# Ten blocks by seven products instead of nine, with the ordinary work spread evenly over their half units

## The chip, the cores and the metric

The kernel runs on one core of a Trainium2 chip. The metric is the device time of one execution in microseconds; the median of several runs is compared. TensorE (PE in the profile) multiplies, VectorE (DVE) and ScalarE (ACT) do elementwise work, GpSimd (POOL) and SyncE (SP) issue transfers.

## The reference

Two decoder layers on x of 256 tokens by 2048, in float32. Each layer mixes tokens (a gated unit and windowed attention), and then comes the part that matters here, a gated feed-forward of width 5632:

```python
h2 = rms_norm(x, norm2_g[l])
x = x + (jax.nn.silu(h2 @ w_gate[l]) * (h2 @ w_up[l])) @ w_down[l]
```

## The kernel before, in words

**Three products for one.** Each float32 weight tile is split into a rounded high half `wh` (a cast on ScalarE, L95) and the rest `wl` (a subtraction on VectorE, L96), in `split2`. The activations are split likewise when they are made. `mm3` (L133) then issues three matmuls of 128x512: high by high (L134), high by low (L135), low by high (L136). There are five buffers of `wh`, four of `wl`, seven of `raw`, the weights as loaded by `raw_load` through SP's queue.

**Ordinary units.** `unit` loads one weight tile of 256 rows by 512 columns, splits it and multiplies it with both token halves: 12 matmuls, one split. In the feed-forward an ordinary gate-and-up block of 512 columns (`gate_up`, through `even`) is 16 units, 8 for w_gate and 8 for w_up; the down product (`down`) of one block is 8 units, over the four column blocks of the output, and two or three blocks are gathered in one pass of `down`. These accumulate in the two PSUM banks of the pool `pd`. `down` starts each output block with a ScalarE copy of the residual into PSUM (L686) and ends it with a copy back (L705).

**Blocks by seven products.** `seven(b)` computes gate and up of a block together. The two token halves, the two halves of the contraction and the pair gate/up make a product of 2x2 by 2x2 sub-matrices, which Winograd's form does with seven products instead of eight. Its half units, `s_unit`, have 6 matmuls and one split each. Five PSUM banks of the pool `pa` hold the five running results (`bank[0]` to `bank[4]`). Sums of weight tiles are made by VectorE (L605, L606, L611; 128x1024 each) and in one case by a transfer that adds while it writes (L613, issued by GpSimd); sums of activations are made once per layer in `combine`. In the first part four rounds of five half units are issued; then the banks are combined on VectorE (L624 to L629); in the second part four rounds of two half units add the products with `b21` to bank 0 and with the kept tiles `t2` to bank 2. At the end L638 adds bank 2 to `m0`, ScalarE applies silu (L641), VectorE gates (L643), and `act_later` has the result transposed two and three ticks later (`act_T`: four transposes, a cast at L554, a subtraction at L555). A tick is one ordinary unit or two half units.

**The order.** Instructions are issued from Python in the order of two generators. `s_stream` gives the half units of all blocks in `S_BLOCKS` and yields after each, and once more after the sums from PSUM and after the end of a block: 30 times per block. `std_stream` gives the ordinary units: `gate_up` of the other blocks, and `down` as soon as two blocks have their transposed pairs (`CHUNK`); it yields False if nothing is ready. A planner joins them: `vec` adds the assumed VectorE time of what was issued to `debt`, `pe` takes off the assumed TensorE time times `LOAD`, and after each half unit ordinary units are issued while the debt is positive:

```python
for _ in s_stream():
    while debt[0] > 0.0 and next(other, False):
        pass
```

What is left of the ordinary units follows after the last block. The tile framework then places the instructions on the engines; its order on one engine can differ from the order of issue.

Of the kernel before, what the change touches and what calls it, by code (L numbers as in the profile page):

```python
# [12 lines left out]
F32 = mybir.dt.float32  # L13
# [3 lines left out]
ALU = mybir.AluOpType  # L17
# [3 lines left out]
P = 128  # L21
D = 2048
SEQ = 256
NTOK = SEQ // P
# [10 lines left out]
NB = 512  # L35
# [3 lines left out]
NI = 3584 // NB  # L39
NFF = DFF // NB  # L40
ND = D // NB
S_BLOCKS = (2, 3, 4, 5, 6, 7, 8, 9, 10)
GU_BLOCKS = tuple(b for b in range(NFF) if b not in S_BLOCKS)
CHUNK = (2, 3)
ACT_TILES = 8
VEC = 1.14
VEC_P = 0.6
MM = 0.227
LOAD = 0.93
WARM = 12  # L50
UNIT_AT = (6, 9, 12, 15, 19, 23)

# [12 lines left out]
def trunk(ctx, tc, x, xt, w_in, w_out, w_gate, w_up, w_down, sgu_w, sgu_g, consts,  # L65
          band, out):
    nc = tc.nc
# [4 lines left out]
    zp = ctx.enter_context(tc.tile_pool(name="zp", bufs=8))  # L72
# [6 lines left out]
    def f(t):  # L79
        return t.bitcast(F32)  # L80

    def raw_load(src, parts=1):
        raw = wp.tile([P, 2, NB], F32, tag="raw", name="raw", bufs=7)
        n = 2 // parts
        for i in range(parts):
            nc.sync.dma_start(raw[:, i * n : (i + 1) * n, :], src[:, i * n : (i + 1) * n, :])
        return raw

    def split2(raw):
        wh = wp.tile([P, 2, NB], F32R, tag="wh", name="wh", bufs=5)  # L90
        wl = wp.tile([P, 2, NB], F32R, tag="wl", name="wl", bufs=4)
        step = 2 if clock[0] > 1 else 1
        for j in range(0, 2, step):
            src = raw[:, j : j + step, :]
            nc.scalar.copy(wh[:, j : j + step, :], src)  # L95
            nc.vector.tensor_tensor(  # L96
                wl[:, j : j + step, :], src, f(wh[:, j : j + step, :]), ALU.subtract
            )
        vec(1)
        return wh, wl  # L100

    clock = [0]
    debt = [0.0]

    def vec(n, cost=VEC):
        debt[0] += n * cost

    def pe(n):
        debt[0] -= n * MM * LOAD

    serial = itertools.count()
    pending = []

# [3 lines left out]
    def tick(w=1.0):  # L117
        clock[0] += w
        due = sorted((e for e in pending if e[0] <= clock[0]), key=lambda e: e[:2])
        pending[:] = [e for e in pending if e[0] > clock[0]]  # L120
        for e in due:
            e[2]()
# [10 lines left out]
    def mm3(acc, ah, al, wh, wl, first, last, again=False):  # L133
        nc.tensor.matmul(acc, ah, wh, start=first, stop=False, skip_group_check=again)  # L134
        nc.tensor.matmul(acc, ah, wl, start=False, stop=False, skip_group_check=again)  # L135
        nc.tensor.matmul(acc, al, wh, start=False, stop=last, skip_group_check=again)  # L136

    def unit(src, acts, acc, first, last, again=False):
        raw = raw_load(src, 2 if clock[0] < 4 else 1)
        wh, wl = split2(raw)  # L140
        for j in range(2):
            act, aj = acts[j]
            for t in range(NTOK):
                ts = slice(t * P, (t + 1) * P)
                mm3(
                    acc[t], act[:, 0, aj, ts], act[:, 1, aj, ts], wh[:, j, :], wl[:, j, :],
                    first and j == 0, last and j == 1, again,
                )
        pe(12)
        tick()  # L150

    def product(srcs, pairs):
# [98 lines left out]
    for lay in range(L):  # L251
# [298 lines left out]
        def act_T(b, c, sg, pairs_f=pairs_f):  # L550
            ps = pm.tile([P, 2, SEQ], F32, tag="sm", name="ps_f")
            transpose_pair([sg[t][:, 2 * c * P : (2 * c + 2) * P] for t in range(NTOK)], ps)
            pair = tp.tile([P, 2, 2, SEQ], F32R, tag="aT", name="aT")
            nc.scalar.copy(pair[:, 0], ps)  # L554
            nc.vector.tensor_tensor(pair[:, 1], ps, f(pair[:, 0]), ALU.subtract)  # L555
            vec(1, VEC_P)
            pe(2)
            pairs_f.setdefault(b, []).append(pair)

        held = []  # L560
# [15 lines left out]
        def seven(b, lay=lay, pairs2=pairs2, ext2=ext2, act_later=act_later):  # L576
            bank = [pa.tile([P, NB], F32, tag="acc", name=f"m{i}") for i in range(5)]

            def s_unit(raw, m, i, op, first, last, bank=bank):
                wh, wl = split2(raw)  # L580
                for j in range(2):
                    ah, al = (op(2 * i + j, h) for h in range(2))
                    mm3(
                        bank[m], ah, al, wh[:, j, :], wl[:, j, :], first and j == 0,
                        last and j == 1, m in (0, 2),
                    )
                pe(6)
                tick(0.5)

            def a_op(k, t):  # L590
                return lambda p, h: pairs2[p][:, h, k, t * P : (t + 1) * P]

            def e_op(n):
                return lambda p, h: ext2[p][:, h, n, :]

            kept = []
            for i in range(4):
                b11 = raw_load(w_gate[lay, b, i, 0])
                b12 = raw_load(w_up[lay, b, i, 0])
                b22 = raw_load(w_up[lay, b, i, 1])  # L600
                t2 = ap.tile([P, 2, NB], F32, tag="spt", name="t2", bufs=4)
                first, last = i == 0, i == 3
                s_unit(b11, 0, i, a_op(0, 0), first, last)
                yield
                nc.vector.tensor_tensor(b11, b11, b12, ALU.add)  # L605
                nc.vector.tensor_tensor(t2, b11, b22, ALU.add)  # L606
                s_unit(b11, 1, i, e_op(1), first, last)
                vec(1)
                vec(1)
                yield  # L610
                nc.vector.tensor_tensor(b12, b12, b22, ALU.add)  # L611
                s_unit(t2, 3, i, e_op(2), first, last)
                nc.gpsimd.dma_start(t2, w_gate[lay, b, i, 1], accum_op=ALU.add)  # L613
                vec(1)
                yield
                s_unit(b22, 4, i, e_op(3), first, last)
                yield
                s_unit(b12, 2, i, e_op(0), first, last)
                yield
                kept.append(t2)  # L620
            m0, c12, c21, c22 = (
                zp.tile([P, NB], F32, tag="z", name=v) for v in ("m0", "c12", "c21", "c22")
            )
            nc.scalar.copy(m0, bank[0])  # L624
            nc.vector.tensor_tensor(m0, bank[3], m0, ALU.add)
            nc.vector.tensor_tensor(c12, bank[1], m0, ALU.add)
            nc.vector.tensor_tensor(c12, bank[4], c12, ALU.add)
            nc.vector.tensor_tensor(c21, bank[2], m0, ALU.add)
            nc.vector.tensor_tensor(c22, bank[1], c21, ALU.add)  # L629
            vec(5, VEC_P)  # L630
            yield
            for i in range(4):
                b21 = raw_load(w_gate[lay, b, i, 1])
                s_unit(b21, 0, i, a_op(1, 0), False, i == 3)
                yield
                s_unit(kept[i], 2, i, a_op(1, 1), False, i == 3)
                yield
            nc.vector.tensor_tensor(m0, bank[2], m0, ALU.add)  # L638
            sg = [zp.tile([P, NB], F32, tag="z", name="sg0"), m0]
            for t, c in ((0, bank[0]), (1, m0)):  # L640
                nc.scalar.activation(sg[t], c, AF.Silu, scale=rstd2[t])  # L641
            for t, c in ((0, c12), (1, c22)):
                nc.vector.scalar_tensor_tensor(sg[t], c, nrstd2[t], sg[t], ALU.mult, ALU.mult)  # L643
            vec(3, VEC_P)
            act_later(b, sg)
            yield

# [2 lines left out]
        def s_stream(seven=seven):  # L650
            for b in S_BLOCKS:
                yield from seven(b)
# [10 lines left out]
        def gate_up(b, even=even, act_later=act_later):  # L663
            acc = yield from even(b, w_gate)
            sg = []
            for t in range(NTOK):
                s = zp.tile([P, NB], F32, tag="z", name="sg")
                nc.scalar.activation(s, acc[t], AF.Silu, scale=rstd2[t])
                sg.append(s)
            acc = yield from even(b, w_up)  # L670
            for t in range(NTOK):
                nc.vector.scalar_tensor_tensor(
                    sg[t], acc[t], rstd2[t], sg[t], ALU.mult, ALU.mult
                )
            vec(NTOK, VEC_P)
            act_later(b, sg)

        left = [NFF]
# [45 lines left out]
                    yield False  # L724

        other = std_stream()
        debt[0] = 0.0
        for _ in s_stream():
            while debt[0] > 0.0 and next(other, False):
                pass  # L730
        seven_done[0] = True
        for went in other:
            if not went:
# [91 lines left out]
```

## Time and profile before

| | |
|---|---|
| median of 3 runs | 1953.2 us (1952.04 to 1955.46) |
| the profiled execution | 1952.96 us, span 1951.2 us |
| granted TensorE clock, mean | 0.999 |
| TensorE busy | 1936.5 us (99%), 8884 matmuls |
| VectorE busy | 1624.8 us (83%) |
| ScalarE busy | 1253.2 us (64%) |
| read from HBM | 418.47 MB, 216 GB/s |

Busy times are shares of the span. A group of the profile is named by its line, engine and operation, then output<-input. `m` is a bank of `seven`, `dacc` a bank of the ordinary units, `acc` a bank of `pa` used otherwise, `ps_f` the transposes of the feed-forward, `t` the tile `t2`. A matmul's row lasts longer than the step from one matmul to the next.

### The profile page before, as it was taken

To read this page: it belongs to the slowest core of one execution; us is meant where nothing else is said; L and a number is where in the kernel's file an instruction comes from. 1 tells how busy PE (TensorE), PEld (TensorE's weight loads), DVE (VectorE), ACT (ScalarE), POOL (GpSimd) and SP (SyncE) were. 2 spreads that over 40 slices of the span, in tenths; PEclk is the share of its full clock that TensorE was granted. 3 is DMA by queue.
4 is the path that set the end of the run, shared out by engine and by line. 5 is a ranking of instruction groups with operands and counts; after the bars stand their busy time and mean duration, and the time that the engine had idled before them with its cause. 6 is when DMAs were issued, how large, how long until landed. Compare 5 with 4: busy or idle time off the path is not lost.

```text
span 1951.2 us, 24946 instructions
## 1 busy us (share of the span) xinstructions
PE 1936.5 (99%) x8884; PEld 1587.5 (81%) x8884; DVE 1624.8 (83%) x1712; ACT 1253.2 (64%) x1651; POOL 115.3 (6%) x116
## 2 busy tenths in 40 slices
PE   9999999999999999999999999999999999999999
PEld 6788888888888888888887888888888888888887
DVE  6566689999999999999556656899999999999983
ACT  7565566666666666667756755666656666666674
POOL 1210000000000000000002000000000000000000
PEclk9999999999999999999999999999999999999999
DMA  9544557768678678768555355586686787778773
GB/s 358 192 146 153 189 169 227 231 225 264 214 218 268 210 229 254 226 215 262 193 200 192 132 164 181 174 256 214 214 274 205 230 253 228 221 233 247 226 252 116
DMA packets 117804, 422.20 MB, mean 216 GB/s; under 512 B 13104, under 2 KB 13744, under 8 KB 117680
## 3 DMA queue, kind: packets, MB, share of 16 engines
q1 hardware_dynamic: 105264, 375.52, 55.2%
q0 software_dynamic: 12416, 45.09, 12.8%
q8 instruction: 69, 1.13, 0.2%
q14 instruction: 55, 0.45, 0.1%
HBM read 418.47 MB, written 2.10 MB: 216 GB/s over the span
## 4 chain that ended last, share of the span: by engine, by line
PE 91%; DVE 3%; issue 3%; ACT 1%; DMA 1%; POOL 1%; SPq 0%; ACTq 0%; DVEq 0%; POOLq 0%
PE m L135 11%; PE m L136 11%; PE m L134 11%; PE dacc L135 10%; PE dacc L134 10%; PE dacc L136 10%; PE acc L135 8%; PE acc L136 8%; PE acc L134 8%; DVE wl L96 1%; PE ps_f L199 1%; POOL ir L182 1%; PE ps_v L372 1%; PE ps_n L199 1%; ACT s L349 0%
## 5 line engine op out<-in xcount | busy, mean ns | idle before, releaser
L95 ACT CAST wh<-raw 128x1024 fp32r<-128x1024 f32 (+1 forms) x778 | 800.9, 1050 | 530.4 <-DVE raw L605 173.8
L96 DVE TENSOR_TENSOR wl<-raw,wh 128x1024 fp32r<-128x1024 f32 (+1 forms) x778 | 930.4, 1218 | 171.2 <-PE acc L135 98.6
L134 PE MATMUL m<-wh,ext 128*128 128x512 f32 x576 | 226.1, 393 | 0.0
L135 PE MATMUL m<-wl,ext 128*128 128x512 f32 x576 | 224.9, 390 | 1.1 <-DVE wl L96 1.1
L135 PE MATMUL dacc<-wl,aT 128*128 128x512 f32 x576 | 225.9, 392 | 0.0
L136 PE MATMUL dacc<-wh,aT 128*128 128x512 f32 x576 | 225.0, 391 | 0.0
L136 PE MATMUL m<-wh,ext 128*128 128x512 f32 x576 | 224.8, 390 | 0.0
L134 PE MATMUL dacc<-wh,aT 128*128 128x512 f32 x576 | 224.3, 394 | 0.1
L96 DVE TENSOR_TENSOR wl<-t,wh 128x1024 fp32r<-128x1024 f32 x144 | 175.8, 1221 | 28.0 <-PE dacc L135 10.4
L134 PE MATMUL acc<-wh,hT 128*128 128x512 f32 x448 | 179.7, 403 | 1.1 <-ACT wh L95 1.1
L135 PE MATMUL acc<-wl,hT 128*128 128x512 f32 x448 | 176.3, 394 | 1.2 <-DVE wl L96 1.2
L136 PE MATMUL acc<-wh,hT 128*128 128x512 f32 x448 | 175.9, 393 | 0.0
L95 ACT CAST wh<-t 128x1024 fp32r<-128x1024 f32 x144 | 151.2, 1050 | 36.9 <-PE dacc L136 21.9
L134 PE MATMUL m<-wh,hT 128*128 128x512 f32 x432 | 168.4, 390 | 0.0
L136 PE MATMUL m<-wh,hT 128*128 128x512 f32 x432 | 168.3, 389 | 0.0
L135 PE MATMUL m<-wl,hT 128*128 128x512 f32 x432 | 168.3, 389 | 0.0
L134 PE MATMUL acc<-wh,aT 128*128 128x512 f32 x384 | 151.5, 395 | 0.0
L136 PE MATMUL acc<-wh,aT 128*128 128x512 f32 x384 | 150.1, 391 | 0.0
L135 PE MATMUL acc<-wl,aT 128*128 128x512 f32 x384 | 149.7, 390 | 0.0
L613 POOL DMA_DIRECT2D t<-in_w_gate_dram x72 | 61.6, 856 | 1321.3 <-DVE wl L96 1113.1
L135 PEld LDWEIGHTS dacc<-wl,aT 128*128 128x128 f32 x576 | 108.2, 188 | 26.4 <-DVE wl L96 4.7
L134 PEld LDWEIGHTS dacc<-wh,aT 128*128 128x128 f32 x576 | 107.8, 188 | 25.2 <-ACT dacc L686 2.0
(138 smaller groups left out, 2839.4 us busy)
## 6 DMA issues: line engine op xcount, KB each, us to landing
raw<-in_w_gate_dram SPq DMA_DIRECT2D x176, 512.0 KB, 6.0
raw<-in_w_up_dram SPq DMA_DIRECT2D x176, 512.0 KB, 4.4
raw<-in_w_down_dram SPq DMA_DIRECT2D x176, 512.0 KB, 4.8
raw<-in_w_in_dram SPq DMA_DIRECT2D x108, 512.0 KB, 4.3
t<-in_w_gate_dram POOLq DMA_DIRECT2D x72, 512.0 KB, 7.0
raw<-in_w_out_dram SPq DMA_DIRECT2D x64, 512.0 KB, 3.4
bias<-in_band_dram POOLq DMA_DIRECT2D x8, 512.0 KB, 4.5
xr<-in_xt_dram SPq DMA_DIRECT2D x8, 256.0 KB, 6.7
```

The source lines that it names most:

```text
L95: nc.scalar.copy(wh[:, j : j + step, :], src)
L96: nc.vector.tensor_tensor(wl[:, j : j + step, :], src, f(wh[:, j : j + step, :]), ALU.subtract)
L134: nc.tensor.matmul(acc, ah, wh, start=first, stop=False, skip_group_check=again)
L135: nc.tensor.matmul(acc, ah, wl, start=False, stop=False, skip_group_check=again)
L136: nc.tensor.matmul(acc, al, wh, start=False, stop=last, skip_group_check=again)
L182: anchor[0] = nc.gpsimd.tensor_tensor(r, ms, mhalf[:, :n], ALU.pow)
L199: nc.tensor.transpose(ps[:, j, t * P : (t + 1) * P], blocks[t][:, j * P : (j + 1) * P], ident)
L372: nc.tensor.matmul(pv[:, r, i], pt[:, (r * n + i) * (t + 1) + b, :], zkv[b][:, cols], start=b == 0, stop=b == t,)
L613: nc.gpsimd.dma_start(t2, w_gate[lay, b, i, 1], accum_op=ALU.add)
```

## The change

Block 1 joins `S_BLOCKS`, so ten blocks go by seven products and only block 0 is ordinary. The planner and its costs go; in their place ordinary units are issued in proportion to the half steps done, with 16 held back for the end. The sum of the lower left result, c21, is made right after the first part and copied by ScalarE into bank 2, so that the second part accumulates onto it; L638 goes, and the silu reads bank 2. In the second part the product with a kept tile is issued one round later than before. The tile `sg0` goes; `m0` and `c21` take the gated results.

```diff
-S_BLOCKS = (2, 3, 4, 5, 6, 7, 8, 9, 10)
+S_BLOCKS = (1, 2, 3, 4, 5, 6, 7, 8, 9, 10)
...
+HALVES = 30 * len(S_BLOCKS)
+STD_UNITS = 8 * NFF + 16 * len(GU_BLOCKS)
+TAIL = 16
...
             nc.scalar.copy(m0, bank[0])
             nc.vector.tensor_tensor(m0, bank[3], m0, ALU.add)
+            nc.vector.tensor_tensor(c21, bank[2], m0, ALU.add)
+            nc.scalar.copy(bank[2], c21)
             nc.vector.tensor_tensor(c12, bank[1], m0, ALU.add)
+            nc.vector.tensor_tensor(c22, bank[1], c21, ALU.add)
             nc.vector.tensor_tensor(c12, bank[4], c12, ALU.add)
-            nc.vector.tensor_tensor(c21, bank[2], m0, ALU.add)
-            nc.vector.tensor_tensor(c22, bank[1], c21, ALU.add)
             yield
-            for i in range(4):
-                b21 = raw_load(w_gate[lay, b, i, 1])
-                s_unit(b21, 0, i, a_op(1, 0), False, i == 3)
-                yield
-                s_unit(kept[i], 2, i, a_op(1, 1), False, i == 3)
-                yield
-            nc.vector.tensor_tensor(m0, bank[2], m0, ALU.add)
-            sg = [zp.tile([P, NB], F32, tag="z", name="sg0"), m0]
-            for t, c in ((0, bank[0]), (1, m0)):
+            for i in range(5):
+                if i < 4:
+                    b21 = raw_load(w_gate[lay, b, i, 1])
+                    s_unit(b21, 0, i, a_op(1, 0), False, i == 3)
+                    yield
+                if i > 0:
+                    s_unit(kept[i - 1], 2, i - 1, a_op(1, 1), False, i == 4)
+                    yield
+            sg = [m0, c21]
+            for t, c in ((0, bank[0]), (1, bank[2])):
                 nc.scalar.activation(sg[t], c, AF.Silu, scale=rstd2[t])
...
         other = std_stream()
-        debt[0] = 0.0
-        for _ in s_stream():
-            while debt[0] > 0.0 and next(other, False):
-                pass
+        done = 0
+        for k, _ in enumerate(s_stream()):
+            while done * HALVES < (k + 1) * (STD_UNITS - TAIL) and next(other, False):
+                done += 1
```

More of the change, by code (lines that the diff above doesn't have):

```diff
@@ L45 @@
 ACT_TILES = 8
[L46 to L49, printed above, removed]
+HALVES = 30 * len(S_BLOCKS)
+STD_UNITS = 8 * NFF + 16 * len(GU_BLOCKS)
+TAIL = 16
 WARM = 12
@@ L98, in split2 @@
             )
-        vec(1)
         return wh, wl
     clock = [0]
[L103 to L109, printed above, removed]
     serial = itertools.count()
@@ L148, in unit @@
                 )
-        pe(12)
         tick()
@@ L555, in act_T @@
             nc.vector.tensor_tensor(pair[:, 1], ps, f(pair[:, 0]), ALU.subtract)
-            vec(1, VEC_P)
-            pe(2)
             pairs_f.setdefault(b, []).append(pair)
@@ L586, in s_unit @@
                     )
-                pe(6)
                 tick(0.5)
@@ L607, in seven @@
                 s_unit(b11, 1, i, e_op(1), first, last)
-                vec(1)
-                vec(1)
                 yield
@@ L613, in seven @@
                 nc.gpsimd.dma_start(t2, w_gate[lay, b, i, 1], accum_op=ALU.add)
-                vec(1)
                 yield
@@ L625, in seven @@
             nc.vector.tensor_tensor(m0, bank[3], m0, ALU.add)
+            nc.vector.tensor_tensor(c21, bank[2], m0, ALU.add)
+            nc.scalar.copy(bank[2], c21)
             nc.vector.tensor_tensor(c12, bank[1], m0, ALU.add)
+            nc.vector.tensor_tensor(c22, bank[1], c21, ALU.add)
             nc.vector.tensor_tensor(c12, bank[4], c12, ALU.add)
-            nc.vector.tensor_tensor(c21, bank[2], m0, ALU.add)
-            nc.vector.tensor_tensor(c22, bank[1], c21, ALU.add)
-            vec(5, VEC_P)
             yield
-            for i in range(4):
-                b21 = raw_load(w_gate[lay, b, i, 1])
-                s_unit(b21, 0, i, a_op(1, 0), False, i == 3)
-                yield
-                s_unit(kept[i], 2, i, a_op(1, 1), False, i == 3)
-                yield
-            nc.vector.tensor_tensor(m0, bank[2], m0, ALU.add)
-            sg = [zp.tile([P, NB], F32, tag="z", name="sg0"), m0]
-            for t, c in ((0, bank[0]), (1, m0)):
+            for i in range(5):
[8 more added lines that the diff above has]
+            for t, c in ((0, bank[0]), (1, bank[2])):
                 nc.scalar.activation(sg[t], c, AF.Silu, scale=rstd2[t])
@@ L643, in seven @@
                 nc.vector.scalar_tensor_tensor(sg[t], c, nrstd2[t], sg[t], ALU.mult, ALU.mult)
-            vec(3, VEC_P)
             act_later(b, sg)
@@ L674, in gate_up @@
                 )
-            vec(NTOK, VEC_P)
             act_later(b, sg)
```

## The prediction

> **What bounds the kernel now.** I read the page first, then the busy time by stretches, then VectorE and TensorE in order of time around one block, and last the waits of the first layer's seven-product stretch (291 to 897 us). The page: span, engines, chain.
>
> ```profile
> span 1951.2 us, 24946 instructions
> PE 1936.5 (99%) x8884; PEld 1587.5 (81%) x8884; DVE 1624.8 (83%) x1712; ACT 1253.2 (64%) x1651; POOL 115.3 (6%) x116
> PE 91%; DVE 3%; issue 3%; ACT 1%; DMA 1%; POOL 1%; SPq 0%; ACTq 0%; DVEq 0%; POOLq 0%
> ```
>
> TensorE carries 91% of the chain. The page warns that its busy share is modelled, so the pace of matmuls counts. Two rows of the timeline, the first and the twelfth matmul of one ordinary unit:
>
> ```profile
> 407.25 0.39 PE L134 MATMUL dacc<-wh,hT 128*128 128x512 f32 x1
> ...
> 409.75 0.39 PE L136 MATMUL dacc<-wh,hT 128*128 128x512 f32 x1
> ```
>
> Eleven steps in 2.50 us: **0.227 us a matmul**, though each row lasts 0.39. An ordinary unit (12 matmuls) is 2.72 us, a half unit (6) is 1.36. Now the stretches: one block (the products end one block apart), then the ordinary work behind the last block; the columns are PE, PEld, DVE, ACT, POOL, granted clock, DMA share, GB/s.
>
> ```profile
> 407.00:476.00 69.00, 69.00 (x308) 56.77 (x307) 66.14 (x62) 42.88 (x47) 3.43 (x4) 1.00 0.75 235
> 828.00:897.00 69.00, 69.00 (x308) 56.62 (x308) 64.99 (x61) 47.42 (x57) 3.41 (x4) 1.00 0.75 233
> 942.00:965.00 23.00, 23.00 (x103) 19.07 (x102) 9.83 (x9) 16.11 (x25) 0.00 (x0) 1.00 0.57 186
> ```
>
> Within a block VectorE is busy 65 to 66 of 69 us; behind the last block 9.8 of 23. So TensorE bounds the stage, VectorE stands right behind it, and ScalarE (43 to 47) and the DMA (0.75) have room. What VectorE costs TensorE today is in the waits of 291 to 897 us:
>
> ```profile
> PE m L135 <- DVE wl L96: 0.6, 1, 0.6
> PEld dacc L135 <- DVE wl L96: 3.4, 9, 0.4
> PEld m L135 <- DVE wl L96: 1.2, 2, 1.0
> DVE wl L96 <- PE dacc L135: 8.7, 17, 1.5
> DVE wl L96 <- issue: 4.0, 5, 1.3
> DVE aT L555 <- ACT aT L554: 3.1, 6, 0.6
> DVE wl L96 <- ACT wh L95: 2.0, 6, 0.6
> ```
>
> TensorE waits 0.6 + 3.4 + 1.2 = 5.2 us for VectorE over nine blocks, 0.58 a block, 10.4 in both layers. Where that comes from is seen on VectorE at a block's end:
>
> ```profile
> 352.04 1.22 DVE L96 TENSOR_TENSOR wl<-t,wh 128x1024 fp32r<-128x1024 f32 x1
> 353.39 1.23 DVE L96 TENSOR_TENSOR wl<-raw,wh 128x1024 fp32r<-128x1024 f32 x1
> 354.75 1.23 DVE L96 TENSOR_TENSOR wl<-t,wh 128x1024 fp32r<-128x1024 f32 x1
> 356.12 1.23 DVE L96 TENSOR_TENSOR wl<-raw,wh 128x1024 fp32r<-128x1024 f32 x1
> 357.38 1.23 DVE L605 TENSOR_TENSOR raw<-raw 128x1024 f32<-128x1024 f32 x1
> 358.64 1.23 DVE L606 TENSOR_TENSOR t<-raw 128x1024 f32<-128x1024 f32 x1
> 359.80 1.23 DVE L96 TENSOR_TENSOR wl<-raw,wh 128x1024 fp32r<-128x1024 f32 x1
> 360.94 0.68 DVE L638 TENSOR_TENSOR m<-m,m 128x512 f32<-128x512 f32 x1
> 361.54 0.74 DVE L643 SCALAR_TENSOR_TENSOR sg<-c,nr,sg 128x512 f32<-128x512 f32 x1
> 362.20 1.22 DVE L96 TENSOR_TENSOR wl<-raw,wh 128x1024 fp32r<-128x1024 f32 x1
> 363.34 0.74 DVE L643 SCALAR_TENSOR_TENSOR m<-c,nr,m 128x512 f32<-128x512 f32 x1
> ```
>
> From 352 to 356 the splits start 1.36 apart, TensorE's pace: VectorE is ahead and waits for one of four `wl` buffers. It can be some three units ahead, about 3 us among half units. From 357.38 to 364 come two adds of the next block, L638 and two gatings, 1.26 + 1.16 + 0.60 + 2 x 0.66 = 4.3 us without a split, and the lead is spent: these are the 0.58 us.
>
> **The change part by part.** *Block 1 goes to seven products.* In each layer 16 ordinary units (192 matmuls) go and 28 half units (168) come: 24 fewer. Two layers: 48 x 0.227 = **10.9 us off** TensorE, all on the bounding engine. Its transposes stay.
>
> *What it adds on VectorE.* VectorE's prices are start to start (timeline; the last row is from the chain in order of time):
>
> ```profile
> 408.01 4.62 DVE L96 TENSOR_TENSOR wl<-raw,wh 128x1024 fp32r<-128x1024 f32 x4
> 412.55 0.68 DVE L625 TENSOR_TENSOR m<-m,m 128x512 f32<-128x512 f32 x1
> 413.27 0.69 DVE L626 TENSOR_TENSOR c<-m,m 128x512 f32<-128x512 f32 x1
> 417.19 0.68 DVE L628 TENSOR_TENSOR c<-m,m 128x512 f32<-128x512 f32 x1
> 417.78 1.21 DVE L96 TENSOR_TENSOR wl<-t,wh 128x1024 fp32r<-128x1024 f32 x1
> 404.00 0.68 DVE L555 TENSOR_TENSOR aT<-ps_f,aT 128x512 fp32r<-128x512 f32 x1
> 404.61 1.22 DVE L96 TENSOR_TENSOR wl<-raw,wh 128x1024 fp32r<-128x1024 f32 x1
> 794.63 0.44 PE ps_f L199 x4
> ```
>
> A split is 4.54 / 4 = 1.135; a 512-wide operation 0.60, or 0.72 where the next one needs its result; the transposed pair 0.61, with 0.44 on TensorE. L605 is 1.26, L606 1.16 and L611 like a split; the split in front of L605 is 0.12 longer (356.12 to 357.38). A block's own VectorE work: 28 splits 31.8, that 0.12 four times 0.5, adds 4 x (1.26 + 1.16 + 1.135) = 14.2, sums from PSUM after the change 0.72 + 4 x 0.60 = 3.1, gatings 1.3, pairs 1.2: 52.1.
>
> *Ordinary work spread evenly.* A layer has 104 ordinary units now (88 down, 16 for block 0); 16 are held for the end, so 88 go over 300 half steps, 8.8 a block. VectorE: 52.1 + 8.8 x 1.135 = **62.1 us a block**. TensorE: (168 + 8.8 x 12) x 0.227 + 2 x 0.44 = **63.0**. Before, a block of 69 us with about 11 ordinary units had 52.1 + 0.6 (L638) + 12.5 = 65.2 on VectorE: a reserve of almost 4 us, which shrinks to 0.9. It decides the case.
>
> Inside a block after the change: in the first part each of four rounds has five half units and 1.47 ordinary ones. VectorE 5 x 1.135 + 0.12 + 3.56 + 1.67 = 11.0, TensorE 6.8 + 4.0 = 10.8: 0.2 us of lead is lost a round, 0.8 in all. The PSUM sums then cost 3.1. In the second part VectorE needs 8 splits and 2.9 of ordinary ones, 12.4, against 18.9 on TensorE: 6.5 comes back. Room for the lead is three units less the split in work, 3.1 among half units and 4.4 with one ordinary unit among them. If the sums run in one lump, about 6.5 must be held in 4.4 and some 2 us are lost to full buffers, 1.1 beyond the reserve. If they are spread among splits, nothing is. The timeline above has splits between them (L626 at 413.27, L628 not before 417.19), so I take the spread, and the block's end, which loses L638 (0.60), as costing what it costs now: 0.58 a block, bounds 0 and 1.7. The tenth block adds 2 x 0.58 = **1.2**.
>
> *A hole.* Ordinary unit 17 is asked for at half step 55, but block 0's pairs need three ticks more, six half units at 0.5. So some seven half units stand alone around the end of the second block: VectorE 7 x 1.135 + 1.3 + 2.4 + 0.1 = 11.8, plus four pairs 2.4, against 9.5. The 4.7 lost meets about 3.1 of lead: bounds 0 and 2 a layer, I take 1.2, **2.4** in both. The three units that then catch up cost VectorE little.
>
> *Lower left result.* L638 goes, L628 moves up, and a copy of c21 into bank 2 comes on ScalarE.
>
> ```profile
> L624 ACT COPY m<-m 128x512 f32<-128x512 f32 x18 | 10.4, 577 | 0.0
> t<-in_w_gate_dram POOLq DMA_DIRECT2D x72, 512.0 KB, 7.0
> 358.71 1.05 ACT L95 CAST wh<-raw 128x1024 fp32r<-128x1024 f32 x1 [2.73 <-DVE raw L605]
> ```
>
> 0.58 us, covered by ScalarE's idle third. The copy waits for c21, which waits for the last product of the first part; behind it stand ScalarE's casts, and the first kept unit on TensorE waits for it. In between TensorE has two half units and at least one ordinary one, 2.7 + 2.7 = 5.4 us (ordinary units stand 3.4 half steps apart); the chain is 0.72 + 0.58 and a 1.14 split and a 1.05 cast in front, 3.5. Zero, if the copy is queued where its input is due; below zero is excluded, nothing waits for bank 2 today. Bank 0, last written two half units before the end instead of one, comes free earlier.
>
> *Loads.* Per layer POOL's queue gets four more (7.0 us to land, needed a part later); SP's stay at 16 for the block, re-ordered. At 0.75 DMA share: zero.
>
> **Sum:** -10.9 + 1.2 + 2.4 = -7.3 us. The profiled execution took 1952.96 us, 1.8 over its span and 0.2 under the median 1953.2: **1946**.
>
> *A rule against it.* The Trainium skill, "VectorE: DVE Perf Modes", section "The DRAIN you can't avoid", says that a VectorE operation starts only when the pipe behind the last has emptied. By that rule a split would take its full row, 1.22, and a block some 66 us on VectorE: 50 to 60 us slower in all. The trace disagrees, four splits start 1.135 apart, so it gets no chance of its own.
>
> **The rivals.** *VectorE becomes the bound.* TensorE would wait in the first part and behind the PSUM sums. For: the reserve of 0.9; VectorE's own waits (4.0 + 3.1 + 2.0 = 9.1 us in nine blocks, 1.0 a block), harmless with 4 us of reserve, would count. Against: the lead recovers in every second part. Price: 2.0 lost to full buffers + 1.0 - 0.9 = 2.1 a block, 42 in all against 10.4: -10.9 + 31.6 gives 1974; half of it 1958; middle 1965. It decides from (10.9 + 10.4) / 20 = 1.07 us of waits a block, where the gain is gone. Chance 0.24.
>
> *The gain is just eaten:* 0.8 to 1.1 us a block, 1950 to 1957. Chance 0.10.
>
> *The copy holds ScalarE.* If it is queued ahead of casts before c21 is due, they stand as the cast at 358.71 did, 2.7 us behind L605; beyond the cover that is 1 to 2 us a block, 20 to 40: 1966 to 1986. Chance 0.05. The Trainium skill, "PSUM — Partial Sum Buffer", section "Engine vs sequencer instructions", calls ScalarE's queue strict FIFO; the waiting cast agrees.
>
> *The waits vanish:* without L638 and with ordinary units in the second part the block's end costs nothing: 1952.96 - 10.9 - 5 to 10 = 1932 to 1937. Chance 0.06.
>
> **How the numbers follow.** The forecast has 0.55, its own range 1941 to 1949. A measurement tells about 0.2%, 3.9 us, from no change. Faster: 0.55 + 0.06 = 0.61; same 0.13 (the eaten gain and the weakest of VectorE's bound); slower 0.26. 1939 to 1964 leaves out most of the vanishing waits and the dearer half of VectorE's bound, under 0.2.
>
> **What would show it.** Right: 48 matmuls fewer at 0.227; blocks about 63.6 us apart; VectorE 62 us or more of each; TensorE's waits for `wl` near 6 to 7 us a layer; 16 ordinary units behind the last block; the copy in bank 2 waited for by nobody. Wrong: blocks 65 us apart or more, with waits of L135 for L96 spread over the first part; or casts waiting behind the copy.

## The result and the profile after

The changed kernel takes 1949.21 us (median of 11 runs, 1948.33 to 1951.0), the kernel before on the same chip 1953.5: ratio 0.998, interval 0.997 to 0.9989. It is faster by 4.3 us, the way that was forecast, by a little over half of the 7.3 us forecast. The page after, its first lines and the chain:

```profile
span 1947.2 us, 25055 instructions
PE 1929.0 (99%) x8836; PEld 1577.2 (81%) x8836; DVE 1657.5 (85%) x1752; ACT 1304.9 (67%) x1729; POOL 122.1 (6%) x124
PE 91%; issue 3%; DVE 3%; ACT 2%; POOL 1%; DMA 1%; SPq 0%; ACTq 0%; DVEq 0%; POOLq 0%
```

8836 matmuls stand for 8884: the 48 are gone. VectorE and ScalarE have more to do, as they should. For the rest I use one number for each kernel: its **gaps**, the sum over the stretch from the first to the last matmul of the seven products of a layer of what each step exceeds its pace by (0.227 us behind a 512-wide matmul, 0.109 behind a transpose), from the timeline. Before, 4.9 and 4.7 us in the two layers; after, 8.7 and 9.1. So -48 x 0.227 = -10.9 and 8.1 more of gaps leave -2.8 us; measured were 3.9 (by the ratio) to 4.3, with an interval of 2.1 to 5.9. Over the whole span the gaps grow by 6.9 us, which leaves -4.0, as the two profiled spans differ (1951.2 and 1947.2). Half of the gaps of a layer lie in one place. Stretches of the changed kernel's first layer (PE, PEld, DVE, ACT, POOL, granted clock, DMA share, GB/s):

```profile
405.00:415.00 10.00, 10.00 (x49) 8.28 (x49) 9.27 (x11) 6.27 (x9) 0.00 (x0) 1.00 0.47 155
415.00:419.00 4.00, 2.02 (x10) 1.11 (x9) 4.00 (x5) 2.49 (x4) 0.00 (x0) 0.98 0.00 0
419.00:423.00 4.00, 4.00 (x12) 2.90 (x12) 4.00 (x5) 3.95 (x5) 0.00 (x0) 0.59 0.63 184
423.00:433.00 10.00, 10.00 (x48) 8.24 (x47) 8.31 (x9) 3.74 (x5) 0.85 (x1) 1.00 0.95 277
440.00:500.00 60.00, 60.00 (x269) 49.44 (x268) 57.79 (x55) 42.94 (x50) 2.59 (x3) 1.00 0.76 244
```

From 415 to 419 TensorE works 2.0 of 4 us while VectorE is busy all of them; then, for 3.4 us, the granted clock is half. This is the hole of the prediction, the end of the second block. Together 4.4 us, in both layers. What VectorE does there, in order of time:

```profile
412.74 1.22 DVE L95 TENSOR_TENSOR wl<-raw,wh 128x1024 fp32r<-128x1024 f32 x1
414.69 0.75 DVE L627 SCALAR_TENSOR_TENSOR c<-c,nr,c 128x512 f32<-128x512 f32 x1 [0.73 <-ACT c L625]
415.36 1.22 DVE L591 TENSOR_TENSOR raw<-raw 128x1024 f32<-128x1024 f32 x1
416.50 0.68 DVE L544 TENSOR_TENSOR aT<-ps_f,aT 128x512 fp32r<-128x512 f32 x1
417.10 1.22 DVE L592 TENSOR_TENSOR t<-raw 128x1024 f32<-128x1024 f32 x1
418.23 2.35 DVE L95 TENSOR_TENSOR wl<-raw,wh 128x1024 fp32r<-128x1024 f32 x2
```

(L95 is the split, L591 and L592 the sums that were L605 and L606, L544 the transposed pair, L627 the gating.) From the end of one split (413.96) to the start of the next (418.23) pass 4.3 us: 3.5 of other work and a wait of 0.7, and no lead meets them. Before, the longest stretch without a split at a block's end was 2.4 us (the rows from 357.38 to 359.80 in the prediction). ScalarE in the same place:

```profile
413.97 0.69 ACT L625 ACTIVATE c<-m,ir 128x512 f32<-128x512 f32 x1 [2.09 <-PE m L126]
416.67 2.00 ACT L94 CAST wh<-raw 128x1024 fp32r<-128x1024 f32 x2 [1.51 <-DVE raw L591]
```

So a chain runs through three engines: the silu (L625) waits for the block's last product, VectorE's gating (L627 at 414.69) waits for the silu, the next block's first sum (L591) stands behind the gating, and ScalarE waits 1.5 us for that sum to cast it. TensorE in order of time:

```profile
415.31 0.40 PE L126 MATMUL m<-wh,hT 128*128 128x512 f32 x1
417.23 0.33 PE L188 MATMUL ps_f<-ident,m 128*128 128x128 f32 x1 [1.53 <-DVE aT L544]
...
417.77 0.50 PE L124 MATMUL m<-wh,ext 128*128 128x512 f32 x1
418.71 1.12 PE L124 MATMUL dacc<-wh,aT 128*128 128x512 f32 x2 [0.45 <-ACT wh L94]
...
420.09 0.63 PE L126 MATMUL m<-wh,ext 128*128 128x512 f32 x1
420.52 0.63 PE L124 MATMUL m<-wh,ext 128*128 128x512 f32 x1
```

The transposes wait for the subtraction of the pair in front, which holds the one bank of `ps_f`. The matmul behind them, at 417.77, needs the cast of the sum, which starts at 416.67 and takes about 1 us (two take 2.00), so it could not have begun before 417.7 anyway. Then matmuls step by 0.43. The other blocks lose little, as the row of 440 to 500 shows: 269 matmuls and transposes in 60 us with VectorE at 57.8. TensorE's waits over the whole stretch (289 to 929 us):

```profile
PE ps_f L188 <- DVE aT L544: 1.5, 1, 1.5
PE dacc L124 <- ACT wh L94: 0.4, 1, 0.4
PE m L124 <- ACT wh L94: 0.3, 1, 0.3
PEld m L125 <- DVE wl L95: 3.7, 15, 0.5
PEld ps_f L188 <- DVE aT L544: 2.8, 4, 2.0
PEld dacc L124 <- ACT wh L94: 1.9, 4, 0.8
PEld m L124 <- ACT wh L94: 1.4, 4, 0.8
PEld dacc L125 <- DVE wl L95: 0.4, 2, 0.3
```

Waits for `wl` are 4.1 us in ten blocks where before they were 5.2 in nine.

### The profile page after: what moved, and what is told of

Same layout as the page of the kernel before. It is cut to its first block, busy times and chain, and to the rows that moved or that the text cites. A ratio compares the mean times of both kernels' runs of the same rounds, so it can differ in the third digit from the quotient of the medians.

```text
span 1947.2 us, 25055 instructions
## 1 busy us (share of the span) xinstructions
PE 1929.0 (99%) x8836; PEld 1577.2 (81%) x8836; DVE 1657.5 (85%) x1752; ACT 1304.9 (67%) x1729; POOL 122.1 (6%) x124
## 4 chain that ended last, share of the span: by engine, by line
PE 91%; issue 3%; DVE 3%; ACT 2%; POOL 1%; DMA 1%; SPq 0%; ACTq 0%; DVEq 0%; POOLq 0%
PE m L125 13%; PE m L124 13%; PE m L126 13%; PE acc L125 8%; PE acc L126 8%; PE acc L124 8%; PE dacc L124 8%; PE dacc L125 8%; PE dacc L126 8%; PE ps_f L188 1%; DVE wl L95 1%; POOL ir L171 1%; PE ps_v L361 1%; ACT wh L94 1%; PE ps_n L188 1%
## 5 line engine op out<-in xcount | busy, mean ns | idle before, releaser
L95 DVE TENSOR_TENSOR wl<-raw,wh 128x1024 fp32r<-128x1024 f32 (+1 forms) x786 | 934.2, 1218 | 170.9 <-PE acc L125 92.7
L125 PE MATMUL m<-wl,ext 128*128 128x512 f32 x640 | 253.0, 395 | 0.3 <-DVE wl L95 0.2
L124 PE MATMUL m<-wh,ext 128*128 128x512 f32 x640 | 251.8, 395 | 0.7 <-ACT wh L94 0.7
L126 PE MATMUL m<-wh,ext 128*128 128x512 f32 x640 | 250.7, 392 | 0.0
L95 DVE TENSOR_TENSOR wl<-t,wh 128x1024 fp32r<-128x1024 f32 x160 | 194.6, 1220 | 2.2 <-issue 1.3
L94 ACT CAST wh<-t 128x1024 fp32r<-128x1024 f32 x160 | 168.5, 1053 | 34.4 <-PE m L126 14.2
L125 PE MATMUL m<-wl,hT 128*128 128x512 f32 x480 | 187.2, 390 | 0.0
L126 PE MATMUL m<-wh,hT 128*128 128x512 f32 x480 | 187.2, 390 | 0.0
L124 PE MATMUL m<-wh,hT 128*128 128x512 f32 x480 | 185.8, 389 | 0.0
L597 POOL DMA_DIRECT2D t<-in_w_gate_dram x80 | 68.4, 855 | 1331.0 <-DVE wl L95 1188.7
L125 PEld LDWEIGHTS m<-wl,ext 128*128 128x128 f32 x640 | 120.7, 189 | 32.2 <-DVE wl L95 7.9
L124 PEld LDWEIGHTS m<-wh,ext 128*128 128x128 f32 x640 | 120.5, 188 | 27.4 <-ACT wh L94 2.7
```

The lines of the kernel that those rows point to most:

```text
L95: nc.vector.tensor_tensor(wl[:, j : j + step, :], src, f(wh[:, j : j + step, :]), ALU.subtract)
```

## The experiments

Theory 1: the gain is lost in the hole and elsewhere where VectorE's reserve is short. Rival: the reserve costs everywhere, and a filled hole only moves the wait. All times are ratios to the kernel before, run on the same chip, with 95% intervals; gaps are per layer, first and second, from the one profiled execution of each.

| run | ratio | gaps, us |
|---|---|---|
| before | 1 | 4.9, 4.7 |
| the change | 0.998 (0.997 to 0.9989) | 8.7, 9.1 |
| e1_no_hole | 0.9969 (0.9957 to 0.9981) | 6.2, 6.6 |
| e2_late_pairs | 0.9978 (0.9969 to 0.9988) | 8.6, 8.9 |
| e3_old_finish | 1.0024 (1.0015 to 1.0034) | 12.6, 12.5 |
| e4_nine_even | 0.9975 (0.9965 to 0.9985) | 2.5, 2.5 |
| e5_nine_planner_new | 0.9999 (0.9991 to 1.0008) | 4.0, 4.3 |
| e6_pool_add | 1.015 (1.0136 to 1.0164) | 24.1, 25.3 |
| e7_tail10 | 0.9963 (0.9951 to 0.9976) | 5.0, 5.1 and 1.5 behind |
| e9_nine_even_new | 0.9968 (0.9955 to 0.998) | 1.5, 1.5 |
| e10_tail12 | 0.9969 (0.9958 to 0.9981) | 8.0, 7.9 |
| e11_tail24 | 0.9951 (0.9939 to 0.9964) | 5.7, 5.7 |
| e12_first_part_only | 0.997 (0.996 to 0.998) | 2.3, 2.4 |
| e13_three_ahead | 0.9992 (0.9983 to 1.0001) | 9.2, 10.0 |

The account closes: -10.9 us where there are ten blocks, plus the gaps of both layers less the 9.6 of before, gives every row within its interval (for e7 with the 1.5 behind the stretch), from +28.8 us (e6, measured +1.5% of 1953, 29) to -9.2 (e11, measured -0.49%, 9.6).

**e1: no hole.** `down` may begin with one block.

```diff
-                if len(full) >= CHUNK[0] or rest:
+                if len(full) >= CHUNK[0] or rest or (full and not gus and (not downed or seven_done[0])):
```

> The changed kernel, with the first pass of down allowed to take a single block (and again behind the last block), so that ordinary units never run out inside the half steps; the matmuls are the same. Theory 1 (the gain is lost where ordinary units are missing, 4.4 us of extra matmul gaps a layer at about 409 to 429 us of the changed kernel): the gaps there vanish, about -4 us a layer, 1941 us, 0.994 of the kernel before. Rival 1 (the small reserve of VectorE costs TensorE a few us wherever it is short, so that filling one place only moves the wait): gaps of 8 to 9 us a layer remain, spread differently, 1948 to 1950 us.

1946.75 us against 1952.54. The same place in this kernel:

```profile
415.00:419.00 4.00, 4.00 (x21) 3.29 (x20) 3.89 (x5) 1.41 (x4) 0.00 (x0) 1.00 0.21 81
419.00:423.00 4.00, 3.69 (x17) 2.67 (x16) 4.00 (x5) 4.00 (x7) 0.00 (x0) 1.00 0.00 0
```

The stop shrinks to 0.3 us of idleness in 8, the clock stays whole, and the gaps of the 40 us from 410 on fall from 4.3 to 1.6. The hole is shown as the place, and ordinary units as its cure. VectorE goes even longer without a split here, with sums, a pair and a gating from the first of these rows to the second, 4.8 us:

```profile
417.56 1.23 DVE L591 TENSOR_TENSOR raw<-raw 128x1024 f32<-128x1024 f32 x1
...
422.36 2.35 DVE L95 TENSOR_TENSOR wl<-raw,wh 128x1024 fp32r<-128x1024 f32 x2
```

So the side work alone does not stop TensorE when ordinary units lie beside it. But the time falls short of theory 1's 1941 us, and 6 us a layer stay: 1.6 in the first 40 us of the stage, 1.6 here, 3 over the rest.

**e2: one pair later.**

```diff
-                later(2 + c, ready)
+                later(2 + c + (2 if b == 2 else 0), ready)
```

> The changed kernel, with the transposes of block 2 alone two ticks later; the stretch without ordinary units stays as long as it is. Theory 1a (within the hole it is four transposed pairs in a row on the one PSUM bank of ps_f that stop TensorE): most of the 4.4 us a layer goes, 1942 to 1944 us. Theory 1b (the stretch of half units without ordinary work drains the lead of VectorE, and pairs are a detail): under 1.5 us a layer is won, 1946 to 1949 us.

1948.5 us, gaps as before the edit, the half clock too. In the order of TensorE only the last of the four pairs moved, by 24 matmuls; the one that had waited did not. So this run says little on the pairs; e3 says more. The mean granted clock was 1.000 in two of the nine runs, the two shortest (1945.79 and 1946.22 us); by it the half clock was missing there, though the program is the same.

**e3: the old finish at ten blocks.** L624 to L643 of before put back into the changed kernel.

```diff
-            nc.vector.tensor_tensor(c21, bank[2], m0, ALU.add)
-            nc.scalar.copy(bank[2], c21)
...
+            nc.vector.tensor_tensor(m0, bank[2], m0, ALU.add)
```

> The changed kernel with the old finish of a block (L638 of before on VectorE, c21 third, kept unit right behind its b21 unit, no copy into bank 2). If the block's end is what costs TensorE waits (4.3 us without a split before the change), the 0.6 us come back on VectorE at each end: +0.3 to +0.6 us for each of 20 blocks, 1955 to 1961 us. Rival: the even spread has made the block's end harmless whatever the finish, 1949 to 1951 us.

1956.56 us, as the first reading said, and slower than the kernel before. At the place of the hole TensorE stops here too:

```profile
415.70 0.60 PE L188 MATMUL ps_f<-ident,sg 128*128 128x128 f32 x4
418.21 0.51 PE L124 MATMUL m<-wh,ext 128*128 128x512 f32 x1 [1.91 <-ACT wh L94]
```

The transposes are done without a wait, and TensorE stands 1.91 us for the cast of the next block's first sum. So the bank of `ps_f` is not needed for the stop: the chain from the last product through VectorE's finish of the block, the sum and its cast makes it where TensorE has no ordinary units to go on with.

The gaps rise by 3.4 to 3.9 us a layer, spread over most blocks. From 440 to 930 us, TensorE's waits for `wl` stay where they were (2.5 and 0.2 with the new finish), and those for casts rise from 0.7:

```profile
PEld m L124 <- ACT wh L94: 2.7, 8, 0.8
PEld dacc L124 <- ACT wh L94: 2.6, 6, 0.6
PEld m L125 <- DVE wl L95: 2.1, 9, 0.4
```

So at ten blocks the finish is worth 7 us of gaps, and what grows is TensorE's waits for casts, not those for VectorE's `wl`, where I had put its 0.6 us. Why the casts come late was not followed further, so VectorE's 0.6 us may still stand behind them.

**e4: nine blocks, even spread, old finish.** Only the planner is replaced. The edit stands against the changed kernel; the part left out is the old finish of e3.

```diff
-S_BLOCKS = (1, 2, 3, 4, 5, 6, 7, 8, 9, 10)
+S_BLOCKS = (2, 3, 4, 5, 6, 7, 8, 9, 10)
...
-TAIL = 16
+TAIL = 19
```

> Nine blocks by seven products and the old finish, as before; only the spread of ordinary units is the even one, 19 held back. Matmuls as before. There is no hole, since two ordinary blocks are to be computed. Theory 1: the even spread by itself costs TensorE nothing or wins 1 to 2 us a layer against the planner's 4.7 to 4.9 us of gaps: 1949 to 1953 us. Rival 2 (the planner's order is what keeps VectorE ahead; the even order loses some us a layer): 1957 to 1962 us.

1947.98 us against 1952.54, a little below the 1949 to 1953 expected: the spread alone brings as much as the whole change. TensorE's waits for `wl` from 289 to 932 us, where the kernel before has the 3.4, 1.2 and 0.6 quoted in the prediction, are now:

```profile
PEld m L125 <- DVE wl L95: 1.8, 6, 0.4
PEld dacc L125 <- DVE wl L95: 0.5, 2, 0.4
```

**e5: nine blocks, planner, new finish.** The finish of the change put into the kernel before.

```diff
+            nc.vector.tensor_tensor(c21, bank[2], m0, ALU.add)
+            nc.scalar.copy(bank[2], c21)
...
-            nc.vector.tensor_tensor(m0, bank[2], m0, ALU.add)
```

> The kernel before with the new finish of a block alone (c21 copied into bank 2, kept unit one round later, L638 gone); nine blocks and the planner stay. Theory 2 (each block's end costs TensorE what VectorE's 4.3 us without a split exceed the lead by, 0.3 to 0.7 us each): 0.6 us less there takes most of these gaps, 4.8 down to 2 to 3 us a layer, -4 to -5 us, 1948 us. Rival (the ends cost little, since the planner pays the debt back behind them, and the finish only helps where VectorE has no reserve): within 1 us of before, 1951.5 to 1953.5 us.

1951.74 against 1952.71, 0.9999: the rival. With the planner the finish is worth 0.9 and 0.4 us of gaps in the two layers, too little to measure.

**e6: one sum on GpSimd.**

```diff
-                nc.vector.tensor_tensor(t2, b11, b22, ALU.add)
+                (nc.gpsimd if i == 0 else nc.vector).tensor_tensor(t2, b11, b22, ALU.add)
```

> The changed kernel with the sum L592 of the first round of each block made by GpSimd instead of VectorE, 20 in all; the same products. Theory 1b (VectorE's 4.3 us without a split at a block's end, meeting a lead of nothing, are what stops TensorE in the hole at 415 to 419 us, and the half clock behind it follows from the stop): 1.14 us of VectorE less there takes 1 to 3 us of the 4.4 us a layer, 1943 to 1947 us. Rival (it is the pairs waiting for the one bank of ps_f): the gap stays at 4 us or more, 1948 to 1950 us. If GpSimd's sum is slower than its cover, or slows VectorE while it runs, TensorE waits at every block's start: above 1952 us.

1981.57 us, the third branch. The sum's rows on both engines, and who waits:

```profile
L592 DVE TENSOR_TENSOR t<-raw x60: 1214/1224/1227, 303.6 to 1901.6; 128x1024 f32<-128x1024 f32 x60
L592 POOL TENSOR_TENSOR t<-raw x20: 2372/3377/3382, 286.3 to 1865.3; 128x1024 f32<-128x1024 f32 x20
ACT wh L94 <- POOL t L592: 16.7, 9, 2.3
```

GpSimd takes 3.38 us (the median) where VectorE takes 1.22, and ScalarE's cast of the sum waits 1.9 us each time with the other casts behind it. The edit disturbs more than it relieves, so it does not separate the two readings of the hole.

**e7: ten held back.**

```diff
-CHUNK = (2, 3)
+CHUNK = (1, 3)
...
-TAIL = 16
+TAIL = 10
```

> The changed kernel with down allowed to take a single block whenever it is full, and 10 instead of 16 ordinary units held back, so that a block has 9.4 instead of 8.8 of them beside it. Theory 1 (the gaps that remain of 6.2 to 6.6 us a layer without the hole are VectorE's small reserve, 0.9 us a block; it becomes 2.0 us): 3 to 4 us a layer remain, 1941 to 1944 us. Rival (they are the start of the stage and the lumps of single waits, which the reserve does not change): 6 us a layer remain, 1946 to 1948 us.

1944.94 against 1952.71. Gaps of 5.0 in the stretch and 1.5 behind it, where the last pass of `down` waits for its transposes. Between the two expectations.

**e9: nine blocks, even spread, new finish.** On the changed kernel:

```diff
-S_BLOCKS = (1, 2, 3, 4, 5, 6, 7, 8, 9, 10)
+S_BLOCKS = (2, 3, 4, 5, 6, 7, 8, 9, 10)
...
-TAIL = 16
+TAIL = 19
```

> Nine blocks, even spread and the new finish. Theory 2: the even spread alone has brought the gaps to 2.45 us a layer, the new finish can take 1 us more at most, since a block's end no longer stops TensorE: 1946 to 1948 us. Rival: the finish is worth its 0.4 us a block here as it is at ten blocks, 1940 to 1942 us.

1946.41 us: the finish takes 1 us of gaps a layer, as theory 2 said. With e1 (0.9969) beside it (0.9968), the tenth block brought nothing that could be measured even with the hole filled: 10.9 us of matmuls are paid for with 9.8 of gaps. With the hole they are paid for with 14.7.

**e10 and e11: 12 and 24 held back,** with single blocks allowed as in e7.

```diff
-CHUNK = (2, 3)
+CHUNK = (1, 3)
...
-TAIL = 16
+TAIL = 12
```

> As the run with 10 held back, but 12: a single block may go down when it is full, and the last block's transposes are covered again at the end (with 10 the last pass waited 1.5 us a layer there). Reserve of VectorE 1.6 us a block by the prices of the prediction. Theory 1: gaps of about 4 to 5 us a layer in the stretch, none behind it, 1942 to 1945 us. Rival (which single passes fall where matters more than the reserve): 1946 to 1948 us.

```diff
-TAIL = 16
+TAIL = 24
```

> The same with 24 held back, no stretch without ordinary units: 8 ordinary units beside a block, VectorE 61.2 us of work against 60.8 on TensorE. Theory 1 (the reserve decides): the sign has turned, TensorE waits in every block, 0.4 us and what is lost to full buffers, 8 to 14 us of gaps a layer, 1950 to 1962 us. Rival (only holes and the start of the stage cost, the reserve does not): 5 to 6.5 us a layer as with 16, 1945 to 1948 us.

Both go against theory 1. With 12, and a reserve that should be larger than the change's, gaps are 8; with 24, where by my prices VectorE has more to do than TensorE, they are 5.7, and the kernel is the best of all: 1943.83 against 1954.08. Its running blocks, with those of e13 below them:

```profile
540.00:600.00 60.00, 60.00 (x270) 49.71 (x269) 59.74 (x57) 42.88 (x51) 3.41 (x4) 1.00 0.75 241
```

```profile
540.00:600.00 60.00, 59.93 (x266) 48.55 (x265) 59.07 (x56) 41.75 (x50) 3.45 (x4) 1.00 0.74 237
```

In e11 VectorE is busy 59.7 of 60 us and TensorE loses nothing. So the reserve by itself does not decide: VectorE can be full. e10 has more passes of `down` (nine a layer, most with a single block, against six), each with copies on ScalarE, and TensorE's waits for casts in the stretch are 7.6 us there (e11: 5.4); but e7 has nine passes too and gaps of 5.0, so their number alone does not decide either. Of e11's 5.7 us, 2.6 lie in the first 40 us of the stage and 2.3 around the first pass of `down`.

**e12: nine blocks, no ordinary unit in a block's second part.**

```diff
-            while done * HALVES < (k + 1) * (STD_UNITS - TAIL) and next(other, False):
+            while k % 30 < 21 and done * HALVES < (k + 1) * (STD_UNITS - TAIL) and next(other, False):
```

> Nine blocks, even spread, old finish, but no ordinary unit is issued in the second part of a block; those due there follow at the next block's start, as the planner had it. Theory 3 (the even spread wins at nine blocks because ordinary units in the second part let VectorE's lead grow beyond three half units before the block's end): the gaps go back from 2.5 to 4 to 5 us a layer, 1951 to 1953 us. Rival (it wins by spacing ordinary units in the first part, or by avoiding the planner's runs of two and three): 2.5 to 3 us a layer, 1947 to 1949 us.

1948.21 against 1954.08, gaps of 2.3: my reason for the gain of the spread falls. It is not that ordinary units in the second part raise the lead before a block's end. What is left is where they stand in the first part; which of its features counts stays open.

**e13: three ordinary units ahead,** on e11.

```diff
-            while done * HALVES < (k + 1) * (STD_UNITS - TAIL) and next(other, False):
+            while (done - 3) * HALVES < (k + 1) * (STD_UNITS - TAIL) and next(other, False):
```

> The run with 24 held back, and three ordinary units more right at the start of the stage, taken from the end; the pace after that is the same, 8 a block, and block 0's pairs no longer meet block 2's. Theory 4 (not VectorE's reserve in the running blocks but two places cost: the first 40 us with 2.6 us of gaps, where the last transposes of the norm fall, and the place around 410 to 450 us with 2.3 us, where four pairs and the first pass of down meet): gaps from 5.7 down to 2 to 3 us a layer, 1937 to 1940 us. Rival (VectorE is full; what is not lost there is lost a block later): 5 to 6 us a layer remain, 1942 to 1945 us.

1951.38 against 1952.96, worse than either reading. The start was mended (0.1 us of gaps in the first 40 us), the second place only in part (from 410 to 470 us 1.6, where e11 has 2.3), and every running block now loses about 0.9 us: the two rows above, 266 matmuls in 60 us against 270. The order of units within a block is that of e11, but for single matmuls; the passes of `down` begin in the middle of a block instead of at its start. In the profile ScalarE's wait for the first sum differs, from 540 to 660 us, e13 first:

```profile
ACT wh L94 <- DVE raw L591: 23.6, 8, 4.4
```

```profile
ACT wh L94 <- DVE raw L591: 6.7, 5, 4.2
```

While that cast waits, up to 4.4 us, the casts queued behind it wait too, and VectorE, which needs them, is busy 59.07 instead of 59.74. That the wait is the cause, and why the passes bring it, was not tested.

## Why the prediction was right, and where not

- **48 matmuls at 0.227: right.** The page has exactly 48 fewer, the pace is the same.
- **Blocks 63.6 us apart: right.** From the third to the tenth block 63.4 on the average (592.4 to 653.8 the shortest). The 16 units behind the last block, and the copy into bank 2 for which TensorE never waits, are there too.
- **The block's end, 0.58 us a block as today: too dear.** One to three splits stood behind the first of the five sums from PSUM, and the other four came in a row; even so, outside the hole and the first 60 us a layer loses 2.6 us, about 0.3 a block. Two things stand behind it that I had not separated: the even spread, which I had given no gain, is worth 2.4 us a layer at nine blocks (e4), and the finish, which I had given 0.6 us of VectorE, keeps 3.4 to 3.9 us a layer away at ten (e3) but only about 1 at nine (e9) and 0.4 to 0.9 with the planner (e5). The "4.3 us without a split" of the prediction is the sum of the other work; its own rows show two splits within it.
- **The hole, 1.2 us a layer: the step that failed.** It is 4.4. The stretch came as forecast: 49 matmuls, eight half units, with three of the four pairs. The forecast was off in two places. Its 9.5 us of TensorE left out the pairs' transposes, 1.8 by the prediction's own price, so that only 2.9 us would have been lost, which a lead of 3.1 covers. But the lead was not 3.1: VectorE's last split before the stop ended at 413.96, and by 415.5 TensorE had used up what there was, 1.6 us. What stopped it is the chain from the silu through gating, sum and cast, which the prediction did not have. And the stop brought 3.4 us at half the clock, 1.6 of the 4.4, which it did not have either.
- **The start of the stage: a term that was missing.** The first 60 us cost 1.7 and 2.1 us of gaps against 0.3 before; with three units ahead (e13) they cost nearly nothing in the first 40, but 0.9 in the 20 behind.
- **The sum:** -10.9 + 1.2 + 2.4 was forecast; by the gaps it is -10.9 + 8.1, in the hole 8.8, at the start 3.0, and in the rest of the blocks -3.7. The direction rests on the 48 matmuls. That the size came near rests on luck: 6.4 and 3.0 us too little in the hole and at the start meet 4.9 too much in the other blocks. The forecast's own range of 1941 to 1949 was just missed.
- **The signs.** VectorE is busy about 61 us a block (57.8 of 60) where 62 or more was said, and waits for `wl` are 4.1 us where 6 to 7 were.
- **The rivals.** VectorE did not become the bound: e11 has it full and TensorE without gaps. The point of 1.07 us a block was nearly reached all the same (gaps of 0.87 and 0.91 a block), by single places. The copy hardly held ScalarE up: it waited 0.5 us for its input in both layers together, and casts 3.5 us for it; without it (e3) TensorE waits longer for casts, not less. The rule of an empty pipe, as the prediction put it, would make e11's running blocks impossible: VectorE's rows there add up to 63.9 us in 60. The same paragraph of the Trainium skill, "VectorE: DVE Perf Modes", section "The DRAIN you can't avoid", ends with the exception that a next operation that is not held starts earlier, which the prediction left out.

## What to carry to other kernels

Where one engine bounds and another stands right behind it, count single places as well as averages: a lead of a few units hides a 4 us run of side work only where it has not been spent, and a stretch without cover cost here (4.4 us) nearly what all nine blocks of a layer had cost before (4.9). An average reserve decided nothing (59.7 of 60 us busy without a gap, and 59.1 with 0.9 us lost a block); these two runs (e11 and e13) differ in how long ScalarE, between the two engines, waits for VectorE's sums, but that this decides was not tested. And take a change of several parts apart: the spread alone at nine blocks (e4, 0.9975) brings as much as all of it (0.998). The fastest run, ten blocks with 24 units held back (e11, 0.9951), is 0.2% ahead of nine blocks with spread and finish (e9, 0.9968), and their intervals overlap.

## What the hardware showed

The granted clock can fall for short stops. A stop of 2.0 us in 4 (415 to 419; the longest idle stretch 1.53) was followed by 3.4 us at half the clock, at the same place in both layers. Idle stretches of 1.91 and 0.44 us in e3 at the same place were not, and by the granted clock of 1.000 neither was the stop in two of the nine runs of e2. What decides was not found. The Trainium skill, "TensorE: Matmul & The Clock Gate", section "What's actually happening", says that the clock is halved after an idle window of 3.4 us, that the window runs free, and that the two states are half and whole: the length (3.4 us) and the two states agree with this trace, but here TensorE was never idle for a whole window.

Much of the scatter between runs of one kernel is this clock. Of the kernel before, the runs beside the experiments with a mean granted clock of 1.000 had a mean span of 1949.9 us, those with 0.999 of 1951.3, with 0.998 of 1952.8 and with 0.997 of 1954.4. A stretch of 3.4 us at half the clock leaves out 1.7 us of TensorE's work, 0.0009 of the mean. The changed kernel, with two of them in its profile, never had a run above 0.999.

A float32 sum of 128x1024 takes GpSimd 3.38 us in the median (2.37 to 3.38) against VectorE's 1.22 (the rows under e6).
